# Mixing stage of a hybrid decoder layer: TensorE's order written out, the recurrence's steps spread between the matmuls of products

## The chip, the core and the metric

The kernel runs on one core of a Trainium2 chip, in float32 with three-pass products (below). The metric is the device time of one execution in microseconds, the median of several runs. A profiled execution gives the trace from which every row here comes.

## What is computed

One decoder layer on 1024 tokens of width 1024: a half-step feed-forward layer, a mixing stage, a second feed-forward layer, a gated embedding and a last RMSNorm. The change is in the mixing stage. Its reference, cut:

```
proj = rms(x) @ w_in            # q | f | i | og | pool | gate A | gate B
f = lb + (1 - lb) * sigmoid(f_r);  k = 1 - f;  q = silu(q_r);  v = i_r
S_t = diag(f_t) S_{t-1} + k_t outer v_t;  o_t = S_t^T q_t      # 8 heads, 128x128 state
y_a = (rms_per_head(o) * silu(og)) @ w_branch_a
pooled = trailing mean over 2/4/8/16 tokens - token            # 4 groups of 128 channels
y_b = (pooled @ pool_w * pool_scale) @ w_branch_b
x = x + (sigmoid(ga) * y_a + sigmoid(gb) * y_b) @ w_out
```

## The kernel before

Every product of two float32 matrices is three matmuls on halves of the mantissa (`mm3`: high x high, low x high, high x low; lines 150 to 152), each 128x128 by 128x512. A remainder ("low") is one ScalarE copy (line 118) and one VectorE subtraction (line 119).

The input projection is done in pairs of 128-column blocks (`pair`), by a Strassen-Winograd scheme: seven products instead of eight, each of four `mm3`, so 84 matmuls a pair. `pair` loads the two weight blocks `ra` and `rb`, forms their sums on GpSimd (lines 90 and 93), splits them, and then runs products 1, 2, 6, 5 and 7; products 4 and 3 (`rest`) are kept in `waiting` and run behind products 1 and 2 of the next pair. `qf_pair(h)` makes a head's q and f; `v_pair`, `og_pair`, `gate_pair` and `pool_pair` make two blocks each (two heads' v or output gates, two blocks of a merge gate, two pooling groups), and put them in DRAM.

The recurrence, `hgrn(h, half)`, takes 512 tokens of a head, in four chunks of 128. It computes a chunk's scores by levels 1, 2, 4, ..., 64: at each level eight matmul records of 64 columns (line 837) write a PSUM bank `aux`; VectorE takes parts of it over into the score (`copy_predicated`, line 840; for the two last levels ScalarE, line 848) and multiplies q and k by the decays (line 87), and the next level reads these. Around the levels stand the products of a token with itself (line 810), the transposes of v (817) and k (863), the state products k x v (867), the state's four steps on VectorE (876), the output products (885 and 887), the squares on ScalarE (890), the power on GpSimd (162), the scaling (892), and the transposes of the output (898) with the gate (899).

Tiles come from named rooms: `a` 28 buffers of 1024 columns (the layer's input in its seven forms fills all of them), `w` 12 (weights), `q` 4 (q beside k), `u` 8 of 512 (f and the pairs' outputs), `h` 5 of 512. PSUM has three banks `pA`, one `pB`, one `pC`, three `aux`.

The order of the instructions on each engine isn't written by hand: a planner takes, of what is ready by its own estimate of times, what stands first in the source. All loads and stores are issued by SP's queue. In the source, a head's two calls of `hgrn` follow the pairs that they need, and one or two pairs of `others` follow them:

```
qf_pair(0)
for h in range(HEADS):
    if h < HEADS - 1:
        qf_pair(h + 1)
    if h % 2 == 0:
        v_pair(h)
        og_pair(h)
        flush()
    for half in range(2):
        hgrn(h, half)
    others.pop(0)()
    if h in (1, 3):
        others.pop(0)()
```

Behind the loop the pooled groups `m` are loaded and split, `branch_b(j)` multiplies them by a block of `w_branch_b` and by gate B for j = 0 to 7, `load_act` loads the recurrence's outputs for branch A, and four pairs of `w_branch_a` follow, then the product with `w_out`.

Of the kernel before, what the change touches and what calls it, by code (L numbers as in the profile page):

```python
# [16 lines left out]
P = 128  # L17
# [7 lines left out]
NG = 4  # L25
# [12 lines left out]
def hybrid_block(ctx: ExitStack, tc: tile.TileContext, a: dict, out: bass.AP):  # L38
# [102 lines left out]
    def load(dst, src):  # L141
        nc.sync.dma_start(out=dst, in_=src)
        return dst

    def store(dst, src):
        nc.sync.dma_start(out=dst, in_=src)
# [100 lines left out]
    def norm_act(x, which, tr="aux"):  # L247


        act = new_act()  # L250
        b1 = {}
        g = gains[:, which, :]
        ng = ngains[:, which, :]

        xn = []

        def rows():
            xn.extend(normed_rows(x, range(4)))

        def first():  # L260
            for kc in range(KC):
                ps = turned(xn, kc, tr)
                b1[kc] = t_(("u", "h")[kc >= 6], "b1")
                nc.scalar.mul(b1[kc], ps, g[:, kc : kc + 1])
                if kc % 2:
                    act_first(act, b1[kc - 1], b1[kc])

        def second():
            ts = range(4, 8)
            diag = scales(x, ts)  # L270
            yield
            for kc in range(0, KC, 2):
                p12 = turned_by(x, ts, diag, kc)
                b22 = t_("h", "b22")
                nc.scalar.mul(b22, turned_by(x, ts, diag, kc + 1), g[:, kc + 1 : kc + 2])
                act_second(
                    act, b1[kc], b1[kc + 1], p12, b22, g[:, kc : kc + 1], ng[:, kc : kc + 1]
                )
                yield

        return act, rows, first, second
# [7 lines left out]

    def flush():  # L290
        while waiting:
            waiting.pop(0)()

    def pair(wa, wb, act, tiles, on11, on22, on21, on12, early=False):

        c1, c2, c3 = tiles
        w = {}

        def product(i, ps, start):
            s, b = SIDES[i]
            hi, lo = w[s]
            for k in range(4):
                c = slice(k * P, (k + 1) * P)
                mm3(ps, hi[:, c], lo[:, c], *act[b][k], start and k == 0, k == 3)
# [20 lines left out]
        yield  # L327
        pa, pc = bank("pA"), bank("pC")
        product(1, pa, True)
        nc.scalar.copy(c1, pa)  # L330
        product(2, pc, True)
        add(c1, c1, pc)
        on11(c1)
        yield
        if early:
            sums(raw(wa, "ra"), raw(wb, "rb"))
        yield
        flush()
        pb = bank("pB")
        product(6, pa, False)  # L340
        nc.scalar.copy(c2, pa)  # L341
        product(5, pb, True)
        product(7, pa, False)
        nc.scalar.copy(c3, pa)
        add(c3, c3, pb)
        on22(c3)

        def rest():
            product(4, pa, False)
            on21(pa)  # L350
            product(3, pb, False)
            add(c2, c2, pb)
            on12(c2)

        waiting.append(rest)

    def steps(it, n=9):
        for _ in range(n):
            if next(it, 0) == 0:
                return  # L360
# [4 lines left out]
    def run_pair(*args, **kw):  # L365
        if not starts:
            steps(pair(*args, **kw))
            return
# [52 lines left out]
    def ffn_up(act, w1, w3, gs, after=None):  # L421
        chunk = []

        def one(c):
# [13 lines left out]
            run_pair(  # L438
                w1[c], w3[c], act, (g1, g2, c3),
                silu, lambda t: None, lambda ps: mul(g1, g1, ps), on12,  # L440
            )
# [236 lines left out]
    def qf_pair(h):  # L678
# [18 lines left out]
        run_pair(w_in[Q + h], w_in[F + h], act, (qk[0][:, L], qk[1][:, L], f[1]),  # L697
                 q_(0), f_(1), f_(0), q_(1))

    def out_pair(wa, wb, act_, done):  # L700

        c1, c2, c3, c4 = (t_("u", "o") for _ in range(4))
        run_pair(
# [3 lines left out]
        )  # L707

    def v_pair(h):
# [5 lines left out]
        out_pair(w_in[V + h], w_in[V + h + 1], act, done)  # L715

    def og_pair(h):
        def done(i, half, t, src):
# [7 lines left out]
            store(og_dram[h + i][half], t)  # L726

        out_pair(w_in[OG + h], w_in[OG + h + 1], act, done)

    def gate_pair(at, j, dst):  # L730
# [4 lines left out]
        out_pair(w_in[at + j], w_in[at + j + 1], act, done)  # L735

    pw_split = []

    def pool_group(g, u):
# [3 lines left out]
        while sh < win:  # L743
            nxt = [t_("h", "pw"), t_("h", "pw")]
            for half in range(2):
# [16 lines left out]
        if not pw_split:  # L762
            r = t_("h", "pwr")
            load(r.rearrange("p (g d) -> p g d", g=NG), a["pool_w"].rearrange("g c d -> c g d"))
            pw_split.append(hilo_half(r, "w", "pwhl"))
        wh, wl = pw_split[0]
        gc = slice(g * P, (g + 1) * P)
        for half in range(2):
            ph, pl = hilo_half(u[half], "w", "pb")
            ps = bank("aux")  # L770
            mm3(ps, wh[:, gc], wl[:, gc], ph, pl, True, True)
            nc.scalar.mul(u[half], ps, pscale[:, g : g + 1])
            store(m_dram[g][half], u[half])

    def pool_pair(g):
        got = {}

        def done(i, half, t, src):
# [3 lines left out]
            for k in range(2):  # L782
                if (k, 0) in got and (k, 1) in got:
                    pool_group(g + k, [got.pop((k, 0)), got.pop((k, 1))])

        out_pair(w_in[PU + g], w_in[PU + g + 1], act, done)
# [7 lines left out]
    def hgrn(h, half):  # L794
# [3 lines left out]

        qk, f = heads[h][0][half], heads[h][1][half]
# [16 lines left out]
        for p_, v_ in zip(chunks(ps), chunks(v)):  # L816
            nc.tensor.transpose(p_, v_, ident)
        nc.scalar.copy(v, ps)
# [12 lines left out]
        for hh in LEVELS:  # L831
# [3 lines left out]
            for c in range(4):  # L835
                right = qc[c].rearrange("p (a two h) -> p a two h", two=2, h=hh)[:, :, 1, :]
                nc.tensor.matmul(ps[:m, c, :64], kc[c][:, :m], right, start=True, stop=True)  # L837
            if hh < 32:
# [23 lines left out]
        for p_, a_ in zip(chunks(ps)[:need], kc):  # L862
            nc.tensor.transpose(p_, a_, ident)
        nc.scalar.copy(k[:, : need * P], ps[:, : need * P])
        ps = bank("aux")
        for p_, a_, b_ in zip(chunks(ps)[:need], kc, vc):
            nc.tensor.matmul(p_, a_, b_, start=True, stop=True)
        befores = []
        for c, (s_, p_) in enumerate(zip(chunks(t_("h", "st")), chunks(ps))):
# [13 lines left out]
        for c, p_ in enumerate(chunks(ps)):  # L883
            s_ = befores[c]
            nc.tensor.matmul(p_, sc[:, c, :], vc[c], start=True, stop=s_ is None)
            if s_ is not None:
                nc.tensor.matmul(p_, qc[c], s_, start=False, stop=True)
        rs = const.tile([P, 4], F32, tag="rso", name=name("rso"), bufs=2)
# [7 lines left out]
        ps = bank("aux")  # L896
        for p_, a_ in zip(chunks(ps), qc):
            nc.tensor.transpose(p_, a_, ident)
        nc.vector.scalar_tensor_tensor(og, ps, onorm[:, h : h + 1], og, ALU.mult, ALU.mult)
        store(o_dram[h][half], og)  # L900

    others = [
        lambda: gate_pair(GB, 0, gb_dram), lambda: pool_pair(0),
        lambda: gate_pair(GB, 2, gb_dram), lambda: pool_pair(2),
        lambda: gate_pair(GB, 4, gb_dram), lambda: gate_pair(GB, 6, gb_dram),
        lambda: gate_pair(GA, 0, ga_dram), lambda: gate_pair(GA, 2, ga_dram),
        lambda: gate_pair(GA, 4, ga_dram), lambda: gate_pair(GA, 6, ga_dram),
    ]
    qf_pair(0)
    for h in range(HEADS):  # L910
        if h < HEADS - 1:
            qf_pair(h + 1)
        if h % 2 == 0:
            v_pair(h)
            og_pair(h)
            flush()
        for half in range(2):
            hgrn(h, half)
        others.pop(0)()
        if h in (1, 3):  # L920
            others.pop(0)()


    m_parts = []
    for g in range(NG):
        m = t_("q", "m")
        for half, c in enumerate((L, R)):
            load(m[:, c], m_dram[g][half])
        m_parts.append(halves(hilo(m, "a", "m")))

    BANKS_B = ("aux", "aux", "pA", "aux", "pA")
    n_b = [0]

    def branch_b(j):
        r = load(t_("w", "rw")[:, :HALF], a["w_branch_b"][j])
        wh, wl = hilo_half(r, "w", "wb")
        for half, cols in enumerate((L, R)):
            gb = load(t_("h", "gb"), gb_dram[j][half])
            ps = bank(BANKS_B[n_b[0] % len(BANKS_B)], "yb")
            n_b[0] += 1  # L940
# [3 lines left out]
            t = t_("u", "o")  # L944
            mul(t, ps, gb)
            store(yb_dram[j][half], t)
# [25 lines left out]
    for j in range(KC):  # L972
        branch_b(j)
        if j % 2:
            load_act(j // 2)


    for j in range(0, KC, 2):
# [7 lines left out]
        out_pair(a["w_branch_a"][j], a["w_branch_a"][j + 1], act_a, done)  # L986
# [68 lines left out]
    act = rest_of(x)  # L1055

# [130 lines left out]
```

## Time and profile before

| | |
|---|---|
| median of 3 runs | 2464.32 us (2461.43 to 2470.61) |
| the profiled execution | 2467.48 us, span 2465.8 us, mean granted clock 0.979 |
| TensorE matmuls | busy 2346.3 us (95%) |
| VectorE | busy 1482.6 us (60%) |
| ScalarE | busy 975.2 us (40%) |
| GpSimd | busy 446.4 us (18%) |
| DMA | 334.10 MB, 135 GB/s |

A wide matmul's record lasts longer than the step to the next one, so busy TensorE is not TensorE at its peak. The names in rows: PE is TensorE's matmuls, PEld its weight loads, DVE VectorE, ACT ScalarE, POOL GpSimd, SPq the queue that issues DMAs; L837 is line 837 of the kernel before; `out<-in` are the program's tiles.

### The profile page before, as it was taken

How to read it: one execution, taken by the hardware profiler on the slowest of the kernel's cores; microseconds unless marked ns; L12 is line 12 of the kernel's file. 1: busy time of each engine (PE TensorE's matmuls, PEld its weight loads, DVE VectorE, ACT ScalarE, POOL GpSimd, SP SyncE). 2: the span in 40 equal slices, each digit the busy share in tenths (PEclk: the TensorE clock that was granted, in tenths of full speed). 3: DMA queues.
4: the chain of work that ended last, by engine and by line, in shares of the span. 5: the costliest groups of instructions: out<-in, count | busy, mean ns of one | idle time of the engine just before them, and what ended most of it. 6: DMA issues, size and time to landing. Idle time of an engine off the chain costs nothing.

```text
span 2465.8 us, 29423 instructions
## 1 busy us (share of the span) xinstructions
PE 2346.3 (95%) x11003; PEld 1919.4 (78%) x11003; DVE 1482.6 (60%) x2026; ACT 975.2 (40%) x1511; POOL 446.4 (18%) x390
## 2 busy tenths in 40 slices
PE   8899999999998999989999989999899999999997
PEld 5688788888877778768778767777688888888885
DVE  5745555468565665684564675676645544568558
ACT  7433333333554334243333331236433333334654
POOL 2222232100013112122212201201232222100000
PEclk9999999999999999999999988999999999999998
DMA  5244554574232213122312346663225433663323
GB/s 205 88 160 140 176 179 139 177 277 141 90 121 76 90 48 120 56 98 74 107 59 79 117 149 209 221 219 129 98 90 175 154 124 112 211 246 124 109 101 133
DMA packets 133951, 334.10 MB, mean 135 GB/s; under 512 B 15280, under 2 KB 15792, under 8 KB 133808
## 3 DMA queue, kind: packets, MB, share of 16 engines
q1 hardware_dynamic: 133808, 332.23, 39.1%
q8 instruction: 86, 1.41, 0.2%
q14 instruction: 57, 0.47, 0.1%
HBM read 230.98 MB, written 101.19 MB: 135 GB/s over the span
## 4 chain that ended last, share of the span: by engine, by line
PE 80%; DVE 9%; ACT 3%; issue 3%; POOL 2%; DMA 2%; SPq 0%; DVEq 0%; POOLq 0%; ACTq 0%
PE pA L150 12%; PE pA L151 12%; PE pA L152 12%; PE pB L151 6%; PE pB L150 6%; PE pB L152 6%; PE aux L837 4%; PE pC L151 3%; PE pC L152 3%; PE pC L150 3%; PE aux L151 2%; PE aux L152 2%; PE aux L150 2%; DVE qk L87 1%; DVE tot L87 1%
## 5 line engine op out<-in xcount | busy, mean ns | idle before, releaser
L90 POOL TENSOR_TENSOR s<-rb 128x512 f32<-128x512 f32 x74 | 102.4, 1384 | 736.2 <-PE pA L152 359.7
L119 DVE TENSOR_TENSOR wtl<-rb,wth 128x1024 fp32r<-128x1024 f32 x74 | 90.7, 1225 | 152.2 <-ACT wth L118 151.8
L118 ACT CAST wsh<-s 128x1024 fp32r<-128x1024 f32 x74 | 77.8, 1051 | 231.0 <-POOL s L93 219.5
L93 POOL TENSOR_TENSOR rb<-ra,s 128x512 f32<-128x512 f32 x74 | 96.4, 1303 | 382.0 <-DVE wd L119 382.0
L837 PEld LDWEIGHTS aux<-qk 128*128 128x128 f32 (+1 forms) x896 | 107.2, 189 | 44.8 <-issue 28.2
L118 ACT CAST wth<-rb 128x1024 fp32r<-128x1024 f32 x74 | 77.6, 1048 | 155.4 <-POOL rb L93 155.4
L118 ACT CAST gh<-gr 128x1024 fp32r<-128x1024 f32 x84 | 81.8, 980 | 135.8 <-PE aux L151 86.4
L118 ACT CAST wah<-ra 128x1024 fp32r<-128x1024 f32 x74 | 77.9, 1052 | 134.9 <-PE pC L151 81.3
L837 PE MATMUL aux<-qk 128*128 128x64 f32 (+1 forms) x896 | 114.5, 272 | 17.4 <-DVE qk L87 16.5
L119 DVE TENSOR_TENSOR gl<-gr,gh 128x1024 fp32r<-128x1024 f32 x84 | 94.8, 1132 | 59.8 <-ACT gh L118 59.7
L150 PE MATMUL pA<-xT1h,wsh 128*128 128x512 f32 x280 | 111.9, 400 | 19.8 <-ACT xT1h L118 19.8
L119 DVE TENSOR_TENSOR wsl<-s,wsh 128x1024 fp32r<-128x1024 f32 x74 | 91.0, 1230 | 61.8 <-ACT wsh L118 50.4
L150 PE MATMUL pA<-xT3h,wth 128*128 128x512 f32 x296 | 118.1, 399 | 4.2 <-ACT g L341 3.2
L150 PE MATMUL pB<-xT1h,wsh 128*128 128x512 f32 x296 | 117.1, 396 | 1.8 <-ACT xT1h L118 0.9
L150 PE MATMUL pC<-x0h,wah 128*128 128x512 f32 x296 | 117.0, 395 | 1.5 <-ACT x0h L118 1.3
L152 PE MATMUL pA<-x0h,wal 128*128 128x512 f32 x296 | 116.7, 394 | 1.6 <-DVE wal L119 1.6
L152 PE MATMUL pB<-xT1h,wsl 128*128 128x512 f32 x296 | 117.9, 398 | 0.0
L151 PE MATMUL pC<-x0l,wah 128*128 128x512 f32 x296 | 116.8, 394 | 1.0 <-DVE x0l L119 1.0
L151 PE MATMUL pB<-xT1l,wsh 128*128 128x512 f32 x296 | 117.0, 395 | 0.4 <-DVE xT1l L119 0.4
L150 PE MATMUL pA<-x0h,wah 128*128 128x512 f32 x296 | 117.2, 396 | 0.0
L151 PE MATMUL pA<-xT3l,wth 128*128 128x512 f32 x296 | 117.0, 395 | 0.0
L152 PE MATMUL pA<-xT3h,wtl 128*128 128x512 f32 x296 | 117.0, 395 | 0.0
(338 smaller groups left out, 6580.6 us busy)
## 6 DMA issues: line engine op xcount, KB each, us to landing
ra<-in_ffn_w_dram SPq DMA_DIRECT2D x50, 512.0 KB, 3.7
rb<-in_ffn_w_dram SPq DMA_DIRECT2D x44, 512.0 KB, 4.0
gsS<-gs SPq DMA_DIRECT2D x88, 256.0 KB, 2.1
rB<-in_ffn_w_dram SPq DMA_DIRECT2D x40, 512.0 KB, 6.7
gr<-gsS SPq DMA_DIRECT2D x40, 512.0 KB, 3.5
gsA<-g SPq DMA_DIRECT2D x66, 256.0 KB, 2.0
gr<-gsA SPq DMA_DIRECT2D x30, 512.0 KB, 5.1
ra<-in_w_in_dram SPq DMA_DIRECT2D x29, 512.0 KB, 3.6
```

The source lines that it names most:

```text
L87: nc.vector.tensor_tensor(o, x, y, ALU.mult)
L90: nc.gpsimd.tensor_tensor(o, x, y, ALU.add)
L93: nc.gpsimd.tensor_tensor(o, x, y, ALU.subtract)
L118: nc.scalar.copy(hi, src)
L119: nc.vector.tensor_tensor(lo, src, hi.bitcast(F32), ALU.subtract)
L150: nc.tensor.matmul(ps, ah, bh, start=first, stop=False, **kw)
L151: nc.tensor.matmul(ps, ah, bl, start=False, stop=False, **kw)
L152: nc.tensor.matmul(ps, al, bh, start=False, stop=last, **kw)
L837: nc.tensor.matmul(ps[:m, c, :64], kc[c][:, :m], right, start=True, stop=True)
```

## The change

`pair`, `run_pair` and the functions that call them become generators: they stop (`yield False`) behind each of a product's four `mm3`, a "part" of three matmuls. `hgrn` stops behind each of its groups of matmuls, twelve in a half. For each head, `among` draws parts from the pairs that `more` names, so many per group, and within `tc.manual_schedule(engines={nc.tensor.engine})` TensorE's instructions keep the order of the source. The other engines' order stays the planner's.

The pairs are dealt out anew: v, qf and og of head 0 before the loop; in heads 0 and 2 a pooling pair, the next qf pair, the pooling maps and a gate pair; in heads 1, 3 and 5 the next head's v, qf and og; in heads 4 and 6 the next qf pair and two gate pairs; in head 7 two gate pairs and the first column of branch B. The pooling means are taken a step at a time behind each part of a qf pair, in `w` buffers; the maps follow as parts of their own. v of a half is loaded in the half in front of it, behind its eighth group; og of a half behind its state products. The states go into f's tile. The last transposes of a half (`turn`) come behind the third group of the next half. Loads can be queued on SP behind a named transfer (`issue_after`).

```diff
+    behind, latest = [None], [None]
+    def load(dst, src, at_once=False):
+        with ExitStack() as turn:
+            if behind[0] is not None and not at_once:
+                turn.enter_context(tc.issue_after(behind[0]))
+            latest[0] = nc.sync.dma_start(out=dst, in_=src).ins
         return dst
...
             for k in range(4):
                 c = slice(k * P, (k + 1) * P)
                 mm3(ps, hi[:, c], lo[:, c], *act[b][k], start and k == 0, k == 3)
+                yield False
...
-    def pool_group(g, u):
+    def beside_means(it):
+        for part in it:
+            yield part
+            while means and next(means[0], 0) == 0:
+                means.pop(0)
+        while means:
+            for _ in means.pop(0):
+                pass
+
+    def pool_means(g, u):
...
-            nxt = [t_("h", "pw"), t_("h", "pw")]
+            both = t_("w", "pw")
+            nxt = [both[:, L], both[:, R]]
             for half in range(2):
...
                     add(n[:, :sh], c[:, :sh], cur[0][:, HALF - sh :])
+                yield
...
+    def v_of(h, half):
+        return v_next.pop() if v_next else v_load(h, half)
...
-        v = load(t_("h", "v"), v_dram[h][half])
-        og = load(t_("h", "og"), og_dram[h][half])
+        v = v_of(h, half)
 
         ps = bank("aux")
         for p_, k_, q_ in zip(chunks(ps), kc, qc):
             nc.tensor.matmul(p_, k_, q_, start=True, stop=True)
+        yield
...
+        og = load(t_("h", "og"), og_dram[h][half], True)
+        og_last[0] = latest[0]
         befores = []
-        for c, (s_, p_) in enumerate(zip(chunks(t_("h", "st")), chunks(ps))):
+
+        for c, (s_, p_) in enumerate(zip(chunks(f), chunks(ps))):
...
+        def turn():
+            ps = bank("aux")
+            for p_, a_ in zip(chunks(ps), qc):
+                nc.tensor.transpose(p_, a_, ident)
+            nc.vector.scalar_tensor_tensor(og, ps, onorm[:, h : h + 1], og, ALU.mult, ALU.mult)
+            store(o_dram[h][half], og)
+
+        turns.append(turn)
+
+    GROUPS = 2 * 13
+
+    def head(h):
         for half in range(2):
-            hgrn(h, half)
+            for i, _ in enumerate(hgrn(h, half)):
+                if i == 2 and turns:
+                    turns.pop(0)()
+                if i == 7:
+                    at = 2 * h + half + 1
+                    if at < 2 * HEADS:
+                        v_next.append(v_load(at // 2, at % 2))
+                yield
+
+    def among(its, groups, n):
+        parts = (p for it in its for p in it if not p)
+        done = 0
+        for i, _ in enumerate(groups, 1):
+            while done * GROUPS < i * n:
+                next(parts, None)
+                done += 1
+        for _ in parts:
+            pass
+
+    PAIR = 28
...
+    more = {
+        0: lambda: (pool_pair(0), beside_means(qf_pair(1)), pool_maps(),
+                    gate_pair(GB, 0, gb_dram)),
+        2: lambda: (pool_pair(2), beside_means(qf_pair(3)), pool_maps(),
+                    gate_pair(GB, 2, gb_dram)),
+        4: lambda: (qf_pair(5), gate_pair(GB, 4, gb_dram), gate_pair(GB, 6, gb_dram)),
+        6: lambda: (qf_pair(7), gate_pair(GA, 0, ga_dram), gate_pair(GA, 2, ga_dram)),
+        7: lambda: around(gate_pair(GA, 4, ga_dram), act_b(), gate_pair(GA, 6, ga_dram), flushed(),
+                          branch_b(0)),
+    }
...
+    with tc.manual_schedule(engines={nc.tensor.engine}):
+        for h in range(HEADS):
+            its = more[h]() if h in more else (v_pair(h + 1), qf_pair(h + 1), og_pair(h + 1))
+            among(its, head(h), (74 if h == 7 else 3 * PAIR + 4 * (h in (0, 2))))
+        turns.pop(0)()
+    behind[0] = og_last[0]
...
-    for j in range(KC):
-        branch_b(j)
+    for j in range(1, KC):
+        steps(branch_b(j))
         if j % 2:
             load_act(j // 2)
+    behind[0] = latest[0]
```

## Rows read from the trace of the kernel before

**Rows 1.** The page: busy us (share of the span) and instructions of each engine.

```profile
PE 2346.3 (95%) x11003; PEld 1919.4 (78%) x11003; DVE 1482.6 (60%) x2026; ACT 975.2 (40%) x1511; POOL 446.4 (18%) x390
```

**Rows 2.** Timeline of PE, 790 to 840: start us, us, instruction, how many.

```profile
793.22 0.39 PE L150 MATMUL pA<-xT1h,wsh 128*128 128x512 f32 x1
...
801.15 0.39 PE L152 MATMUL pA<-xT3h,wtl 128*128 128x512 f32 x1
...
821.95 0.40 PE L151 MATMUL pB<-xT1l,wsh 128*128 128x512 f32 x1
822.18 1.00 PE L837 MATMUL aux<-qk 128*128 128x64 f32 x8
822.99 0.48 PE L152 MATMUL pB<-xT1h,wsl 128*128 128x512 f32 x1
823.31 0.39 PE L150 MATMUL pB<-xT1h,wsh 128*128 128x512 f32 x1
...
824.45 1.02 PE L837 MATMUL aux<-qk 128*128 128x64 f32 x8
...
828.35 0.39 PE L152 MATMUL pA<-xT3h,wtl 128*128 128x512 f32 x1
...
834.65 0.39 PE L151 MATMUL pA<-x0l,wah 128*128 128x512 f32 x1
...
837.93 0.63 PE L898 MATMUL aux<-ident,qk 128*128 128x128 f32 x4 [0.82 <-DVE tot L87]
...
839.96 0.40 PE L150 MATMUL pC<-x0h,wah 128*128 128x512 f32 x1
```

**Rows 3.** Windows: length; busy (count) PE, PEld, DVE, ACT, POOL; clock, DMA, GB/s.

```profile
801.38:1493.62 692.24, 643.28 (x3490) 529.73 (x3489) 432.68 (x732) 247.26 (x489) 135.65 (x101) 0.98 0.28 91
1403.60:1431.71 28.11, 27.14 (x167) 22.57 (x166) 20.73 (x38) 12.82 (x27) 1.01 (x1) 1.00 0.58 187
1459.80:1493.62 33.82, 22.32 (x102) 19.38 (x101) 20.88 (x38) 8.63 (x19) 1.01 (x1) 0.55 0.28 94
1321.00:1374.00 53.00, 52.40 (x236) 43.37 (x235) 22.39 (x28) 20.39 (x29) 11.88 (x10) 1.00 0.33 104
```

**Rows 4.** The same windows, only instructions on tile aux (PE, PEld, DVE, ACT).

```profile
801.38:1493.62 692.24, 212.54 (x1584) 193.21 (x1583) 97.45 (x183) 55.22 (x216) 0.98 0.28 91
1403.60:1431.71 28.11, 12.17 (x99) 11.31 (x98) 5.99 (x11) 3.09 (x13) 1.00 0.58 187
1459.80:1493.62 33.82, 20.90 (x99) 18.69 (x97) 5.96 (x11) 3.08 (x13) 0.55 0.28 94
```

**Rows 5.** Waits of PE, 740 to 1640: us in total, times, longest.

```profile
PE aux L837 <- DVE qk L87: 16.5, 17, 1.4
PE aux L898 <- DVE qk L892: 15.6, 11, 3.5
...
PE pA L150 <- ACT xT1h L118: 5.9, 1, 5.9
...
PE aux L817 <- DMA v<-v_dram: 1.2, 1, 1.2
```

**Rows 6.** Timeline of DVE around the level group at 822.18.

```profile
823.22 0.44 DVE L840 COPY_PREDICATED score<-mask,aux 128x256 f32<-128x256 uint16 x1 [1.50 <-PE aux L837]
823.56 0.68 DVE L87 TENSOR_TENSOR qk<-qk,tot 128x512 f32<-128x512 f32 x1
```

**Rows 7.** Groups by line, 600 to 1800: busy us, mean ns; idle before.

```profile
L119 DVE TENSOR_TENSOR wtl<-rb,wth 128x1024 fp32r<-128x1024 f32 x34 | 41.6, 1224 | 56.0 <-ACT wth L118 55.6
```

**Rows 8.** DMA issues, 740 to 1500: count, KB each, median us to landing.

```profile
v<-v_dram SPq DMA_DIRECT2D x16, 256.0 KB, 3.0
```

**Rows 9.** Timeline of DVE in a pooling group.

```profile
1066.13 0.68 DVE L81 TENSOR_TENSOR pw<-o 128x511 f32<-128x511 f32 x1
...
1068.81 0.68 DVE L81 TENSOR_TENSOR pw<-pw 128x508 f32<-128x508 f32 x1
```

**Rows 10.** Waits of all engines, 740 to 1640: us in total, times, longest.

```profile
POOL rso L162 <- DVE rso L161: 134.0, 10, 32.7
```

More of the change, by code (lines that the diff above doesn't have):

```diff
@@ L288, in hybrid_block, with flushed @@
     waiting = []
+    def flushed():
+        while waiting:
+            yield from waiting.pop(0)()
     def flush():
-        while waiting:
-            waiting.pop(0)()
+        for _ in flushed():
+            pass
     def pair(wa, wb, act, tiles, on11, on22, on21, on12, early=False):
@@ L348, in rest @@
         def rest():
-            product(4, pa, False)
+            yield from product(4, pa, False)
             on21(pa)
-            product(3, pb, False)
+            yield from product(3, pb, False)
             add(c2, c2, pb)
@@ L357, in steps @@
     def steps(it, n=9):
-        for _ in range(n):
-            if next(it, 0) == 0:
+        for end in it:
+            n -= end
+            if not n:
                 return
@@ L366, in run_pair @@
         if not starts:
-            steps(pair(*args, **kw))
+            yield from pair(*args, **kw)
             return
@@ L702, in out_pair @@
         c1, c2, c3, c4 = (t_("u", "o") for _ in range(4))
-        run_pair(
+        yield from run_pair(
             wa, wb, act_, (c1, c2, c3),
@@ L707, in out_pair @@
         )
+    v_there = set()
     def v_pair(h):
@@ L713, in done @@
             store(v_dram[h + i][half], t)
-        out_pair(w_in[V + h], w_in[V + h + 1], act, done)
+            v_there.add((h + i, half))
+        yield from out_pair(w_in[V + h], w_in[V + h + 1], act, done)
+    og_there, og_last = set(), [None]
     def og_pair(h):
@@ L726, in done @@
             store(og_dram[h + i][half], t)
-        out_pair(w_in[OG + h], w_in[OG + h + 1], act, done)
+            og_there.add((h + i, half))
+        yield from out_pair(w_in[OG + h], w_in[OG + h + 1], act, done)
     def gate_pair(at, j, dst):
@@ L761, in pool_group, with pool_maps @@
             )
[L762 to L773, printed above, removed]
+            yield
+        pooled.append((g, u))
+    def pool_maps():
+        r = t_("h", "pwr")
+        load(r.rearrange("p (g d) -> p g d", g=NG), a["pool_w"].rearrange("g c d -> c g d"))
+        wh, wl = hilo_half(r, "w", "pwhl")
+        while pooled:
+            g, u = pooled.pop(0)
+            gc = slice(g * P, (g + 1) * P)
+            for half in range(2):
+                ph, pl = hilo_half(u[half], "w", "pb")
+                ps = bank("aux")
+                mm3(ps, wh[:, gc], wl[:, gc], ph, pl, True, True)
+                nc.scalar.mul(u[half], ps, pscale[:, g : g + 1])
+                store(m_dram[g][half], u[half])
+                yield False
     def pool_pair(g):
@@ L783, in done, with v_load @@
                 if (k, 0) in got and (k, 1) in got:
-                    pool_group(g + k, [got.pop((k, 0)), got.pop((k, 1))])
-        out_pair(w_in[PU + g], w_in[PU + g + 1], act, done)
+                    means.append(pool_means(g + k, [got.pop((k, 0)), got.pop((k, 1))]))
+        yield from out_pair(w_in[PU + g], w_in[PU + g + 1], act, done)
+    v_next = []
+    def v_load(h, half):
+        assert (h, half) in v_there
+        return load(t_("h", "v"), v_dram[h][half], True)
+    def v_of(h, half):
+        return v_next.pop() if v_next else v_load(h, half)
     states = {}
@@ L895, in hgrn @@
         )
[L896 to L916, printed above, removed]
-        for half in range(2):
-            hgrn(h, half)
-        others.pop(0)()
-        if h in (1, 3):
-            others.pop(0)()
-    m_parts = []
[L925 to L929, printed above, removed]
@@ new lines, in among, with around @@
+    def among(its, groups, n):
[6 more added lines that the diff above has]
+        for _ in parts:
+            pass
+    PAIR = 28
+    def around(first, acts, *its):
+        yield first
+        next(acts)
+        for it in its[:-1]:
+            yield it
+        next(acts)
+        yield its[-1]
+    more = {
[8 more added lines that the diff above has]
+    }
@@ L934, in branch_b, with act_b @@
+    for it in (v_pair(0), qf_pair(0), og_pair(0)):
+        steps(it)
+    m_parts = []
+    def act_b():
+        behind[0] = latest[0]
+        for g in range(NG):
+            m = t_("q", "m")
+            for half, c in enumerate((L, R)):
+                load(m[:, c], m_dram[g][half])
+            m_parts.append(halves(hilo(m, "a", "m")))
+        m_last, behind[0] = latest[0], None
+        yield True
+        behind[0] = m_last
+        yield True
     def branch_b(j):
@@ L937, in branch_b @@
         for half, cols in enumerate((L, R)):
-            gb = load(t_("h", "gb"), gb_dram[j][half])
-            ps = bank(BANKS_B[n_b[0] % len(BANKS_B)], "yb")
-            n_b[0] += 1
+            gb = load(t_("u", "gb"), gb_dram[j][half])
+            ps = bank("pA", "yb")
             for i, g in enumerate((0, 2, 1, 3)):
@@ L943, in branch_b @@
                 mm3(ps, wh[:, c], wl[:, c], *m_parts[g][half], i == 0, i == 3)
-            t = t_("u", "o")
-            mul(t, ps, gb)
-            store(yb_dram[j][half], t)
+                yield False
+            mul(gb, ps, gb)
+            store(yb_dram[j][half], gb)
+    with tc.manual_schedule(engines={nc.tensor.engine}):
[4 more added lines that the diff above has]
+    behind[0] = og_last[0]
     act_a = new_act()
@@ L1055, in hybrid_block @@
     act = rest_of(x)
+    behind[0] = None
     ffn_up(act, a["ffn2_w1"], a["ffn2_w3"], gs_dram,
```

50 lines of the change are left out of this document (28 added, 22 removed).

## The prediction

> **What bounds the kernel now.** The page first: TensorE counts as busy for 95% of the span, VectorE for 60% [rows 1]. Read alone, that leaves 5% to win anywhere. A matmul's record is longer than its pace, though, so I went on to the pace. Where pairs run alone, 36 matmuls of 512 columns start from 793.22 to 801.15, a step of 0.2266 us, while each record says 0.39 [rows 2]; two neighbours can drift apart by 0.16 us and still count as busy. [...]
>
> Then the windows. With pairs alone (1321 to 1374) nothing is lost: 236 matmuls x 0.2266 = 53.5 us for 53.0 [rows 3]. The mixing with the recurrence is another thing. From its first matmul (801.38) to its last (1493.62) are 692.2 us and 3490 matmuls, of which 1584 write aux [rows 3, 4]. 24 of these are pooling maps, which are as wide as the pairs', so 1560 are the recurrence's and about 1930 are wide ones. 1930 x 0.2266 = 437 us. The other **255 us** are what the recurrence's 16 halves cost TensorE, 15.9 each.
>
> How much of that is work? I price one half from the timeline where it runs without idle time [rows 2]. One level group (8 records): from the wide matmul at 821.95 to the second one after it, 823.31, are 1.36, less two steps 0.91. The transposes and first products at a half's start: 837.93 to 839.96, less one step: 1.80. From the last level to the state products, 828.35 to 834.65: 6.30 less the 11 wide matmuls in it (2.49): 3.81. A half is 6 x 0.91 + 1.80 + 3.81 = **11.1 us**, 16 halves 177. So 255 - 177 = **78 us** of the stretch are waits, lost pace and slow clock. [...] A well filled half is the one from 1403.60: 28.1 us, 167 matmuls, 68 of them wide = 15.4, so 12.7 for the recurrence. If all were like it: 203, and 52 us saved.
>
> The waits that TensorE's own list names are the recurrence's: 16.5 us for VectorE's multiply between levels, 15.6 for the normalised output before its transposes [rows 5].
>
> **The change, part by part.** *Order and even spreading.* No matmul is added or taken away. A half has 12 stops for other work; `among` lays 84 parts of three wide matmuls (88 with the maps, 74 counted for the last head) over 26 per head, 3.2 parts between two groups and the rest at the head's end: 3.2 x 3 x 0.2266 = 2.2 us. Does the chain fit into that? After the group at 822.18 the next wide matmul starts at 822.99; VectorE's select starts at 823.22, its multiply ends at 824.24, and the next group starts at 824.45 [rows 2, 6]: 1.46 us. So 0.74 us are spare where VectorE is free. [...] Were everything to fit, the gain would be the 78.
>
> What doesn't fit: VectorE's 1.22 us remainders of weights [rows 7], three per pair, 69 in the 23 pairs of the loop. Against a period of 3.1 us one of them lies in front of the multiply by more than 0.74 now and then: if it gets between select and multiply (0.44 of 3.1) it costs 1.22 - 0.74 = 0.48, if it is running when the select comes due, 0.09 on the mean (0.39 of the time). That is 0.10 x 69 = 7; two such instructions in a row happen, so I take 13. Ends: nothing, and 69 x 0.48 = 33.
>
> *The turn* (transposes of the output) moves to the third group of the next half, 9 us later instead of at once; the chain of squares, power on GpSimd and multiply, of which 3.5 us were the longest wait seen [rows 5], goes under that. The very last one has no cover: 3.
>
> *v a half ahead.* It lands 3.0 us after issue [rows 8]; TensorE waited 1.2 for it, once [rows 5]. The load moves on SP's queue past a half's stores, and its source was stored by the head's first pair long before; og moves back, behind the state products, with a whole gap and three groups until its use. Both at nothing beyond the 1.2, which is in the 78; without that cover, 3.0 per half would show.
>
> *State in f's tile.* Four chunks per half leave the h buffers, but f lives to the end of its head. Two heads' f and an output pair's four tiles fill the eight u buffers; the next pair's first copy needs only the buffer whose store went out a pair ago. Nothing, I estimate.
>
> *Pooling in steps.* A step is one add, 0.67 us apart from the next (1066.13 to 1068.81 for four) [rows 9]; the four groups have 20, and some 1.4 more each, 19 us in all. One step per part asks VectorE for 0.67 beside the pair's 0.285 (22.39 us for 236/3 parts [rows 3]) and the recurrence's 1.19 per group ((20.73 - 22.7 x 0.285)/12) x 0.3 = 0.36: 1.31 us in a part that lasts 0.68 + 0.3 x 0.91 = 0.95. VectorE falls behind by 0.36 over 26 such parts, 9 us; I take 8. Ends: nothing, and all 19. The maps at the end wait some 4 for the last steps.
>
> *Loads behind others.* m's loads, branch B's and branch A's are queued behind a named transfer. Branch A's weights then come only after the last o, some 12 us after the loop; 4 for landing and some 11 for sums and casts end before branch B's seven remaining columns (168 x 0.2266 = 38 us) do. Nothing; without the cover, what exceeds 38.
>
> Sum: 177 + 13 + 3 + 8 + 4 = 205 against 255: **50 us saved**. The profiled execution took 2467.5 us (span 2465.8), 3 above the median of the runs; from the median, 2464.3 - 50 = **2414**.
>
> **Rivals.** *VectorE gives it back.* All three upper ends together: 177 + 33 + 19 + 7 = 236, 19 saved, 2445. For it: VectorE is busy 432.7 of the 692 us already and will have the same work in 640, 68% [rows 3]. Against it: the well filled half runs at 20.73/28.1 = 74% and loses 1.6 us only.
>
> *Slower: GpSimd's queue holds the weights.* The power of each half stands on GpSimd among the sums of the pairs' weights. GpSimd now waits 134 us in ten such places, up to 32.7 at once [rows 10], and TensorE doesn't feel it, since the recurrence's own groups or another pair stand in its order. With the order fixed, a pair whose sums stand behind the power stops recurrence and pairs alike. At 16 powers, 50/16 = 3.1 us each eat the gain; at the 5.9 that TensorE once waited for a cast [rows 5] it is 94: 2464 - 50 + 94 = 2508. Against it: the recurrence's results come at a steady pace, and a pair lasts 26 us instead of 19, so that its sums have 7 more to hide in. [...]
>
> *Nothing happens.* The order by readiness already filled the gaps, and idle time only moves: 2464. Against it: the last half spends 33.8 less three wide matmuls = 33.1 us on the recurrence, 20 more than the well filled one, and the pairs now placed there must change that.
>
> **How the numbers follow.** Forecast, 2390 to 2435 (nothing but the floor, to stalls of 49 in place of 28): 0.62. VectorE gives it back, 2435 to 2455: 0.18. Nothing: 0.08. Slower: 0.12. Half a per cent, 12 us, is about what a measurement of this kernel can tell. Faster by more, under 2452: 0.62 + 0.17 = 0.79; within: 0.01 + 0.08 and 0.01 of the slower case, 0.10; slower: 0.11. The floor is 2464 - 78 = 2386. From 2390 to 2452 hold about 8 in 10.
>
> **What would show it.** Right: the recurrence's groups spread evenly from its first to its last matmul in about 640 us and no half at the low clock; the wait for the normalised output gone; small waits on VectorE's multiply, most of them in the pooling pairs. Wrong: waits of TensorE for casts of weights with GpSimd's power ahead of them; waits for the level multiply at most groups, a microsecond each; or idle time of 10 us and more where branch A begins.

## The result and the profile after

The changed kernel takes **2433.36 us** (median of 4 runs, 2428.49 to 2434.36) against 2463.81 (2461.43 to 2470.61): ratio 0.9868, interval 0.9844 to 0.9892, 30.5 us less. The forecast was 2414, in a range from 2390 to 2452. The profiled executions are 33.7 apart, 2467.48 and 2433.77, since that of before lies above its median.

TensorE's busy time, as the page gives it (compare [rows 1]), fell by 13 us and its share rose by one per cent; it tells little here, as before.

```profile
PE 2333.1 (96%) x11003; PEld 1914.5 (79%) x11003; DVE 1479.2 (61%) x2027; ACT 976.3 (40%) x1512; POOL 446.7 (18%) x390
```

The windows tell more. Line 1 is the stretch from the recurrence's first matmul to its last, as in [rows 3]; then its first half, head 0's second half (pooling), head 2's second half (pooling), a plain half, and the last. The columns are those of [rows 3].

```profile
786.19:1460.28 674.09, 648.98 (x3566) 542.39 (x3564) 430.10 (x731) 249.51 (x496) 141.59 (x105) 0.99 0.28 92
786.19:830.65 44.46, 40.63 (x219) 34.09 (x217) 24.59 (x48) 13.64 (x28) 6.70 (x6) 0.96 0.23 71
830.65:878.53 47.88, 44.29 (x239) 36.63 (x238) 36.00 (x66) 20.26 (x40) 13.04 (x10) 1.00 0.28 94
999.27:1053.89 54.62, 48.22 (x239) 38.34 (x238) 42.41 (x82) 20.19 (x40) 15.01 (x10) 0.94 0.25 83
1092.95:1135.36 42.41, 42.06 (x233) 35.43 (x232) 23.45 (x35) 14.84 (x30) 12.39 (x10) 1.00 0.16 56
1416.02:1460.28 44.26, 39.25 (x214) 32.31 (x212) 31.69 (x48) 19.76 (x38) 1.58 (x2) 0.96 0.64 213
```

Of 3566 matmuls 1560 are the recurrence's, as before, so 2006 are wide: 454.6 us at 0.2266. What is left, called the remainder below, is 674.1 - 454.6 = **220 us** (219.5; 220.0 when each half is taken by itself). It was 255; the forecast had 205, of which 177 are work. The same sum for single halves, with 97 or so matmuls of the recurrence in each:

| half | remainder, us | over the 11.1 of work |
|---|---|---|
| first (786.19) | 16.6 | 5.5 |
| head 0, second (pooling) | 15.9 | 4.9 |
| head 2, second (pooling) | 22.7 | 11.6 |
| last (1416.02) | 19.1 | 8.0 |
| the other twelve, mean | 12.1 (11.4 to 12.6) | 1.0 |

The last half, which cost 33 us when it stood bare, costs 19; the plain ones are at 12.1 on the mean, and of before none was under 12.7. The waits of PE from 730 to 1640 answer to [rows 5]: total, times, longest.

```profile
PE aux L886 <- DVE qk L87: 11.6, 15, 2.7
PE pA L157 <- ACT xT1h L118: 7.4, 2, 4.6
PE aux L865 <- DMA v<-v_dram: 3.8, 1, 3.8
...
PE aux L158 <- DVE pb L119: 2.4, 1, 2.4
...
PE aux L957 <- DVE qk L949: 0.6, 1, 0.6
```

The 15.6 us for the normalised output are 0.6 now. Those for the level multiply are still 11.6, but 8.8 of these stand in the two pooling halves and the last one. The wait for v, 1.2 before, is 3.8. GpSimd waits longer for the power's operand than before ([rows 10]), with no wait of TensorE for a weight behind it in the loop; total, times, longest, from 780 to 1462:

```profile
POOL rso L169 <- DVE rso L168: 170.4, 16, 41.4
```

Outside the stretch the profiled executions differ by little. One pair (84 matmuls, 19.0 us) has moved from ahead of the recurrence into it, and it begins only 15.2 us earlier, so 3.8 were lost there; behind it are 2.4 gained. 35.1 - 3.8 + 2.4 = 33.7.

### The profile page after: what moved, and what is told of

It is laid out like the page before. It is cut to its first block, busy times and chain, and to the rows that moved or that the text cites. A ratio compares the mean times of both kernels' runs of the same rounds, so it can differ in the third digit from the quotient of the medians.

```text
span 2432.0 us, 29361 instructions
## 1 busy us (share of the span) xinstructions
PE 2333.1 (96%) x11003; PEld 1914.5 (79%) x11003; DVE 1479.2 (61%) x2027; ACT 976.3 (40%) x1512; POOL 446.7 (18%) x390
## 4 chain that ended last, share of the span: by engine, by line
PE 75%; DVE 10%; DMA 5%; ACT 3%; issue 3%; POOL 2%; SPq 0%; DVEq 0%; POOLq 0%; ACTq 0%
PE pA L157 12%; PE pA L158 12%; PE pA L159 12%; PE pB L157 6%; PE pB L158 6%; PE pB L159 5%; PE aux L886 3%; PE pC L158 3%; PE pC L159 3%; PE pC L157 3%; PE aux L158 2%; PE aux L159 2%; PE aux L157 2%; DMA rb<-in_ffn_w_dram 1%; DVE tot L87 1%
## 5 line engine op out<-in xcount | busy, mean ns | idle before, releaser
L157 PE MATMUL pA<-xT1h,wsh 128*128 128x512 f32 x280 | 115.5, 412 | 21.4 <-ACT xT1h L118 21.4
L886 PE MATMUL aux<-qk 128*128 128x64 f32 (+1 forms) x896 | 110.4, 266 | 16.3 <-DVE qk L87 11.6
L157 PE MATMUL pB<-x,wth 128*128 128x512 f32 x296 | 118.1, 399 | 0.0
L158 PE MATMUL pA<-x0l,wah 128*128 128x512 f32 x296 | 115.6, 391 | 2.4 <-DVE x0l L119 2.4
L159 PE MATMUL pC<-x0h,wal 128*128 128x512 f32 x296 | 116.6, 394 | 0.0
```

The lines of the kernel that those rows point to most:

```text
L157: nc.tensor.matmul(ps, ah, bh, start=first, stop=False, **kw)
L158: nc.tensor.matmul(ps, ah, bl, start=False, stop=False, **kw)
L159: nc.tensor.matmul(ps, al, bh, start=False, stop=last, **kw)
```

## The experiments

The times are medians; where a ratio stands, it is that to the kernel before, timed beside it. Remainders are computed as above, with 454.6 us for the wide matmuls.

**The fixed order taken away.**

```diff
-    with tc.manual_schedule(engines={nc.tensor.engine}):
+    with ExitStack():
```

> The changed kernel, but TensorE's order is left to the planner again; source, spreading, pairs, loads and pooling steps stay as changed. If the even spreading in the source does the work and the fixed order only holds it, the planner, which takes what stands first in the source of what is ready, comes close to the same order: time within 6 us of the changed kernel's 2433, remainder of the recurrence (stretch from its first to its last matmul less 0.2266 us per wide matmul) 214 to 226 against 220. If the fixed order itself does it, the planner draws the recurrence's groups together again: remainder back towards 255, time some 2465.

Measured: 2419.19, ratio 0.982 (0.9805 to 0.9834): 14 us *faster* than with the fixed order, outside both expectations. Windows: the stretch, head 2's second half, the last half; and the wait for v.

```profile
785.26:1444.49 659.23, 641.82 (x3566) 538.04 (x3565) 434.45 (x732) 250.83 (x496) 139.47 (x105) 1.00 0.29 95
993.30:1043.10 49.80, 45.17 (x239) 36.09 (x238) 43.65 (x82) 20.38 (x40) 13.16 (x10) 1.00 0.26 91
1402.91:1444.49 41.58, 37.77 (x214) 31.12 (x213) 31.82 (x49) 20.34 (x38) 1.58 (x2) 1.00 0.72 235
```

```profile
PE aux L865 <- DMA v<-v_dram: 1.2, 1, 1.2
```

The remainder is 204.6. The plain halves are what they were (12.0). The difference is in the disturbed ones: the first 16.6 to 12.4, pooling 22.7 to 17.9 and 15.9 to 15.2, the last 19.1 to 16.2. At the first half one can see how. In the changed kernel, v is late and TensorE stands:

```profile
789.59 0.39 PE L159 MATMUL pA<-x0h,wal 128*128 128x512 f32 x1
793.81 0.77 PE L865 MATMUL aux<-ident,v 128*128 128x128 f32 x4 [3.83 <-DMA v<-v_dram]
794.23 0.78 PE L157 MATMUL pC<-x0h,wah 128*128 128x512 f32 x1
794.80 0.63 PE L158 MATMUL pC<-x0l,wah 128*128 128x512 f32 x1
...
797.36 0.52 PE L158 MATMUL pC<-x0l,wah 128*128 128x512 f32 x1
```

The planner put ten more wide matmuls in front of the transposes, the last of them at 790.92, and the wait is 1.2:

```profile
788.65 0.39 PE L159 MATMUL pA<-x0h,wal 128*128 128x512 f32 x1
788.88 0.39 PE L157 MATMUL pC<-x0h,wah 128*128 128x512 f32 x1
...
790.92 0.39 PE L157 MATMUL pC<-x0h,wah 128*128 128x512 f32 x1
792.50 0.66 PE L865 MATMUL aux<-ident,v 128*128 128x128 f32 x4 [1.20 <-DMA v<-v_dram]
```

**Groups close together, in the fixed order and in the planner's.**

```diff
-    GROUPS = 2 * 13
+    GROUPS = 2 * 22
```

> The changed kernel with the parts of a head laid over 44 instead of 26 groups: 1.9 parts (1.30 us) between two groups instead of 3.2 (2.2 us), the other 38 parts of a head behind its last group. If cover for the chain of 1.46 us between two level groups is what the change bought, TensorE waits at most level groups, 0.16 at the least and up to 1.2 where VectorE is at a weight's remainder: remainder of the recurrence 250 to 265 against 220, time 2460 to 2475. If the filled last head and the fixed order bought it and the spacing doesn't matter, remainder 215 to 227 and 2428 to 2440.

> TensorE's order left to the planner and a head's parts laid over 44 groups (1.30 us between two, less than the chain's 1.46). If spacing is what counts whoever makes the order, the stretch's remainder rises from 205 to between 225 and 255 and the time to 2440 to 2470. If the planner makes up for close groups by putting later parts between them, the remainder stays under 213 and the time under 2427.

Measured: 2475.88 fixed, 2434.46 by the planner (one run each). The stretch of each, and the fixed one's longest wait:

```profile
783.14:1497.42 714.28, 664.36 (x3566) 550.91 (x3564) 429.78 (x729) 248.67 (x494) 137.38 (x105) 0.97 0.26 86
```

```profile
786.56:1458.96 672.40, 649.10 (x3566) 538.88 (x3564) 427.88 (x729) 248.01 (x494) 140.47 (x105) 0.99 0.28 90
```

```profile
PE aux L886 <- DVE qk L87: 31.6, 29, 3.2
```

Remainders 259.7 and 217.8, against 219.5 and 204.6 with 2.2 us between groups. So 0.9 us of cover per group are worth 40 us where the order is fixed and 13 where the planner makes it. The first remainder lies in the range that I had worked out from the chain of 1.46 us (250 to 265; the time is 0.9 above its range), but not by the waits that I had in mind: not 0.16 at most groups, but 31.6 us in 29 of the 112 level groups, up to 3.2 at once. The second fell between my two expectations: the planner makes up for two thirds.

**The transposes of the output earlier.**

```diff
-                if i == 2 and turns:
+                if i == 0 and turns:
```

> The changed kernel with the last transposes of a half behind the first group of the next half instead of the third: 3.1 us of cover instead of 9 within a head (some 7.5 at a head's start). If their place is worth what the prediction says, TensorE waits about 1 us for the normalised output in each of eight halves and more where GpSimd or VectorE is busy: 8 to 15 us slower, 2441 to 2448, and the wait for the scaling (line 949) comes back at 8 to 15 us. If their place doesn't matter: within 2 us of the changed kernel.

Measured: 2433.70, ratio 0.9877 (0.986 to 0.9893), no change in time. The waits moved in the way expected, by less:

```profile
PE aux L886 <- DVE qk L87: 14.5, 22, 1.2
...
PE aux L957 <- DVE qk L949: 4.7, 9, 1.6
```

4.7 us in nine waits came back where I expected 8 to 15. The plain halves grew by 0.6 on the mean, 7 us in all, but the last half and one of the pooling halves became shorter by 3.3 together, the stretch as a whole is 3.4 longer, and the time doesn't show it. The place of the turn is worth some microseconds at most.

**No pooling means.**

```diff
-                    means.append(pool_means(g + k, [got.pop((k, 0)), got.pop((k, 1))]))
+                    pooled.append((g + k, [got.pop((k, 0)), got.pop((k, 1))]))
```

> The changed kernel without the pooling means (the pooling maps are applied to the tokens themselves; all else is done). If the means' steps on VectorE make the long halves of heads 0 and 2, these halves' remainders fall from 15.9 and 22.7 to 12.5 and 15, the stretch by 11 us: 2422. If the splits of the maps (five pairs of copies and subtractions close together) make them, the halves keep 15 and 20 and the time falls by 3 at most.

Measured: 2422.58, ratio 0.983 (0.9816 to 0.9845), as the first theory says, 11 us. The pooling halves have remainders of 13.6 and 13.6 (12.5 and 15 expected), 11.4 less together, and what they keep over a plain half, 1.5 each, goes with the maps and their splits. The first half fell too, by 2.4: its wait for v was 3.0 there, and the granted clock of the whole stretch is 1.00 where it was 0.99.

**The means in a lump.**

```diff
-            while means and next(means[0], 0) == 0:
-                means.pop(0)
+            while means:
+                for _ in means.pop(0):
+                    pass
```

> The changed kernel, fixed order, with a pooling group's means taken all at once in the source instead of a step behind each part. If the steps ease VectorE's load, the long halves of heads 0 and 2 grow from 15.9 and 22.7 us to 18 and 28, the time to 2441. If VectorE is overloaded there in either way and works through what stands first in the source, both stay within 1.5 us, the time within 4 of 2433.

Measured: 2431.80 (one run); the pooling halves have 17.0 and 24.3, 1.1 and 1.6 more, and the first half and the last differ by 0.8 together. The stretch is 3.3 us longer, though the time of this one run isn't. That is nearer to the second theory, with 1.6 just past its 1.5: the steps ease little, VectorE is overloaded there either way.

**v in its own half, in the fixed order and in the planner's.**

```diff
-                    if at < 2 * HEADS:
+                    if False:
                         v_next.append(v_load(at // 2, at % 2))
```

> The changed kernel, fixed order, with v loaded at its own half's start as before. If SP issues the load about when the half's first group is reached, 3 us of transfer and queue stand against some 3 us of cover, and TensorE waits about a microsecond for v in most of the 16 halves: 10 to 25 us slower, 2443 to 2458. If SP runs far enough ahead that a load early in the source lands early anyway: within 3 us of 2433, and the waits for v stay at the 3.8 us of the first half.

> TensorE's order left to the planner, and v loaded at its own half's start. With the fixed order this cost 16 us, in four halves where TensorE waited up to 3.7 us for v. If what the fixed order costs is that nothing can be taken in front of a late operand, the planner hides most of it: these halves rise by 2 at most, the time is under 2425. If v is late whatever the order: 2432 to 2438.

Measured: 2449.38 fixed, ratio 0.9937 (0.992 to 0.9955); 2425.92 by the planner, ratio 0.9836 (0.9813 to 0.9859). The first is 16 us slower by the medians, as the first theory says (the profiled execution, the fastest of the four, 11.1), but TensorE waits for v in four halves, not in most: the first ones of heads 0, 2, 4 and 6. Head 4's first half, fixed and by the planner, and the waits for v of each:

```profile
1137.51:1181.48 43.97, 40.00 (x216) 33.20 (x215) 27.29 (x50) 15.27 (x30) 6.43 (x6) 0.96 0.34 103
```

```profile
1128.84:1169.88 41.04, 39.50 (x217) 33.43 (x216) 26.61 (x50) 15.26 (x30) 6.05 (x6) 0.96 0.35 110
```

```profile
PE aux L865 <- DMA v<-v_dram: 14.3, 4, 3.7
```

```profile
PE aux L865 <- DMA v<-v_dram: 6.7, 4, 1.9
```

With v a half ahead these halves have 12.0 and 11.2; late, 17.5 and 14.5. The fixed order pays 5.5 for it, the planner's 3.3, so it hides less than I expected (2 at most), and its time lies between my two theories.

**Another order of the pairs ahead of the loop**, by the planner and fixed.

```diff
-    for it in (v_pair(0), qf_pair(0), og_pair(0)):
+    for it in (qf_pair(0), og_pair(0), v_pair(0)):
```

> TensorE's order left to the planner, the three pairs before the loop in the order qf, og, v, the means back on VectorE alone. If the two gains add up, the recurrence begins some 6 us earlier than with the planner's order alone (779 against 785), its stretch keeps a remainder of 203 to 206, and the time is 2410 to 2415, 5 to 8 under the 2419. If the earlier start is given back later: 2417 to 2421.

> The changed kernel, fixed order, with the three pairs before the loop in the order qf, og, v. If the late first v (3.8 us) and what it does to the clock are only a part of what the fixed order costs, the first half falls to some 12 us, the recurrence begins 6 us earlier, the pooling halves and the last one stay at 16, 22.7 and 19: 2421 to 2427, still 8 to 13 over the same pairs with the planner's order (2414). If the first v is all of it: 2412 to 2418.

Measured: 2413.72 (5 runs, 2411.86 to 2418.41), ratio 0.9799 (0.9785 to 0.9814), by the planner, and 2420.81, ratio 0.9818 (0.9798 to 0.9839), fixed. The first is as expected; the second is 0.2 under its range, and 7 over the planner's where I had expected 8 to 13. The recurrence begins at 779.88 and 778.86 instead of 785 to 786; v is in time, and the first half's remainder is 11.0 in both. The stretches:

```profile
779.88:1437.54 657.66, 641.56 (x3566) 538.27 (x3565) 430.98 (x722) 249.32 (x494) 139.52 (x105) 1.00 0.30 95
```

```profile
778.86:1446.83 667.97, 647.26 (x3566) 541.68 (x3564) 428.71 (x720) 247.84 (x493) 139.03 (x105) 0.99 0.29 93
```

The new order of the pairs is worth 12.6 us where TensorE's order is fixed and 5.5 where it isn't, so that about half of what the fixed order costs hung on the start. The intervals of the ratios overlap, for the 5.5 as for the 7 us that remain, so these are less sure than the 14 above; the two stretches are 10.3 apart, of which 8 are in the pooling halves (16.0 and 22.2 against 15.2 and 18.0) and the last (19.0 against 15.9). The planner's order with these pairs beats both kernels; it is the best that I have.

**Half of the means on GpSimd, and no parts left at a head's end** (both by the planner, with the pairs in the order qf, og, v).

```diff
-                add(n[:, sh:], c[:, sh:], c[:, :-sh])
+                (pool_add if half else add)(n[:, sh:], c[:, sh:], c[:, :-sh])
```

```diff
-    GROUPS = 2 * 13
+    GROUPS = 2 * 12
```

> TensorE's order left to the planner, the three pairs before the loop in the order qf, og, v, and the wide adds of the second half's means on GpSimd. Against the run with the planner's order alone (2419): the pairs' order gives back the 3.8 us that the changed kernel lost before the loop, if its last pair's gate work on ScalarE and VectorE made that; the means on GpSimd take 7 adds, some 4.7 us, off VectorE in the half of 17.9, which falls by 3 to 5, and by 1 or 2 in the half of 15.2: 2408 to 2413. If GpSimd's adds (1.4 us each) come later than VectorE's would, these halves grow instead, to 20 and more.

> The kernel with the planner's order, the pairs in the order qf, og, v and half of the means on GpSimd, and besides a head's parts laid over 24 groups, as many as there are, instead of 26: 3.5 parts (2.38 us) between two groups, none left at a head's end. If what still waits in the plain halves is VectorE's long instructions against 0.74 us of spare, 0.18 more of it takes 2 to 5 us off the stretch. If the remaining 12 us per half are work, and the spare is enough already, within 1 us; and if the bare parts at a head's end covered the last transposes, 2 to 5 slower.

Measured: 2416.48, ratio 0.9799 (0.9784 to 0.9815), and 2416.25, ratio 0.9801 (0.9785 to 0.9816). The means on GpSimd are a miss: 2408 to 2413 were expected. Head 0's second half kept its 15.2, head 2's rose from 18.0 to 21.4, as the other theory has it, and TensorE waits for means there that it did not wait for before. 24 groups or 26 make no difference: remainders of 207.2 and 207.5. By what I had written down, that would clear VectorE's long instructions in the plain halves; why it settles little is told in the next section.

## Why the prediction was right, and where it was off

The direction held, and the mechanism in the main. The stretch lost waits, lost pace and slow clock, not work; the recurrence is spread evenly; the last half no longer stands bare; the cover between two groups counts, which the close groups show: with 0.16 us less than the chain of 1.46 the fixed order's remainder is 260, where 255 was before. It isn't all of it: with the same close groups the planner's order keeps only 218, 37 less than before, and spreading takes 13 more. So under the planner the greater part came with the new deal of pairs and loads, 21 of it in the last half alone (33 to 12.4); what each piece of that deal brought was not measured by itself. GpSimd's queue, the rival on the other side, did not decide: its waits for the power grew from 134 to 170 us, and no weight was late in the loop. Long VectorE instructions go with GpSimd's sums, which is another matter, told below.

The size was off by 20 us: 50 forecast, 30.5 measured. Three of these lie between the medians and the profiled executions, which are 33.7 apart. The other 16 are in the terms of the sum, over the 177 of work:

| term | forecast | measured |
|---|---|---|
| VectorE's long instructions; measured, all that the plain halves keep | 13 | 12.5 |
| pooling steps and maps | 8 + 4 | 16.5 |
| the end (last turn) | 3 | 8.0 |
| v ("at nothing beyond the 1.2"), first half | 0 | 5.5 |
| ahead of the recurrence | 0 | 3.8 |
| behind it | 0 | -2.4 |

The first row agrees to half a microsecond, and that is luck. The forecast's cause was a weight's remainder in front of the multiply between levels. But in the twelve plain halves TensorE's list has only 5.7 us of waits, 13 of them. The rest of the 12.5 is lost pace, or work that I priced too low; no run parts the two, and the half from 959.99, with no idle time at all, still has 11.4. Of the 5.7 us, 4.6 stand behind VectorE instructions that were long beside something that I had overlooked, GpSimd's sums of weights. A multiply or another product of 512 columns (L87) took 0.67 to 0.74 us in 142 of the 158 cases in the stretch and 1.00 to 1.74 in 16. Each of the 16 started while GpSimd was adding, and ended 0.55 us after that add did. TensorE's waits for VectorE from 1054 to 1416 (nine of the twelve halves; total, times, longest), then two places, each with VectorE, GpSimd and the wait of TensorE:

```profile
PE aux L886 <- DVE qk L87: 2.4, 8, 0.4
PE aux L886 <- DVE tot L87: 1.8, 2, 0.9
...
1270.00 1.74 DVE L87 TENSOR_TENSOR qk<-qk,tot 128x512 f32<-128x512 f32 x1
1269.89 1.30 POOL L93 TENSOR_TENSOR rb<-ra,s 128x512 f32<-128x512 f32 x1 [7.75 <-DVE wd L119]
1271.88 1.08 PE L886 MATMUL aux<-qk 128*128 128x64 f32 x8 [0.34 <-DVE qk L87]
...
1229.16 3.77 DVE L87 TENSOR_TENSOR tot<-tot 128x128 f32<-128x128 f32 x3
1228.82 1.44 POOL L90 TENSOR_TENSOR s<-rb 128x512 f32<-128x512 f32 x1 [11.98 <-PE pA L159]
1230.34 1.29 POOL L93 TENSOR_TENSOR s<-s,ra 128x512 f32<-128x512 f32 x1
1231.59 1.29 POOL L93 TENSOR_TENSOR rb<-ra,rb 128x512 f32<-128x512 f32 x1
1234.01 1.08 PE L886 MATMUL aux<-qk 128*128 128x64 f32 x8 [0.92 <-DVE tot L87]
```

The three small products in the second place (128, 64 and 32 columns) took 0.29, 0.22 and 0.19 us where GpSimd was not adding. Five waits are of the first kind (1.8 us), three of the second (2.7). Eight products of 512 columns started during an add and took 0.68 to 0.74, and no run moved the sums away, so what they cost in all is open. The run with 24 groups doesn't settle it: with the greater cover, TensorE's waits for the multiply between levels were 8.8 us in eight, where they were 4.8 in ten with 26 groups.

The step of the prediction that failed is the one that reckoned the fixed order as a gain alone ("Order and even spreading"). It lists what the spreading buys and charges nothing for holding TensorE to one order. Without the hold the kernel is 14 us faster, at the same source and the same spreading. The remainders put it together (close groups by the planner: one run): new deal of pairs and loads with close groups, by the planner, 255 to 218; even spreading, to 205; the fixed order, back to 220. My second rival did charge the fixed order, but looked for the cost in the wrong place, at GpSimd's power. The halves in which the fixed order costs are those with a late operand: the first v, the pooling maps' splits, and in the last half what waits for VectorE beside its work on m.

v failed in its own right. "Past a half's stores" on SP's queue was right for 15 of the 16 loads. The first has no half in front of it, and stands behind two weight loads, which wait for GpSimd to be done with a weight buffer. What SP waits for most from 760 to 800 (total, times, longest), and its issues in the changed kernel:

```profile
SPq L149 <- POOL rb L93: 15.5, 2, 12.8
...
786.25 0.33 SPq L149 DMA_DIRECT2D ra<-in_w_in_dram  x1
788.59 0.33 SPq L149 DMA_DIRECT2D rb<-in_w_in_dram  x1
788.97 0.42 SPq L149 DMA_DIRECT2D v<-v_dram  x1
```

SP had issued nothing since 770.24. v goes out at 788.97, and the transposes at 793.81 are the first that can use it. A queue that the load is moved past was looked at for the usual half, not for the first one.

Of pooling I had priced the steps and not the splits behind them: five remainders of 0.68 us on VectorE around 1018 to 1022, one of which TensorE awaits for 2.4. The run without means puts 11.4 us on the steps, where I had 8 and 4. The lump agrees with my picture of the deficit (0.36 us per part) in kind: steps or lump, the work is too much for the time. In the last half I had not listed the four splits of m at all; the longest wait there, 2.7 us, is for the first level's multiply, and VectorE's timeline has two of these splits in front of it, the second itself behind a cast:

```profile
1423.19 1.26 DVE L119 TENSOR_TENSOR ml<-m,mh 128x1024 fp32r<-128x1024 f32 x1
1424.36 0.75 DVE L958 SCALAR_TENSOR_TENSOR og<-aux,onorm,og 128x512 f32<-128x512 f32 x1
1425.93 1.23 DVE L119 TENSOR_TENSOR ml<-m,mh 128x1024 fp32r<-128x1024 f32 x1 [0.82 <-ACT mh L118]
1427.08 0.69 DVE L87 TENSOR_TENSOR qk<-qk,f 128x512 f32<-128x512 f32 x1
```

The 3.8 us ahead of the recurrence have to do with the order of the first three pairs, since another order recovers them; which of these pairs' instructions delays the casts there, I did not separate.

## What to carry to other kernels

Where a chain on one engine alternates with another's work, find the chain's shortest turn (here 1.46 us) and lay a little more cover than that between its steps in the source; that alone was worth 13 us under a planner that may still reorder, and 40 under a fixed order. Look also at what GpSimd does while the chain's VectorE steps run: here one of 0.68 us took up to 1.74 when it started during an add. Try the spreading without the fixed order first: a planner that takes the next thing in the source when one operand is late keeps the gain and loses less at the irregular places, at the start, at the end, and where another stage overloads an engine. When a load is moved ahead, follow it on its queue for the first iteration too.

## What the runs showed of the hardware

After the 3.8 us stand for v (789.59 is the last matmul before it), wide matmuls started 0.43 us apart until 797.4 instead of 0.23. The granted clock was 1.00 up to the stand and in it (785.0 to 793.8) and 0.56 on the mean from 793.8 to 797.4; in windows of 0.4 us it reads 0.50 all the way from 794.6 to 797.4, and 1.00 again from 797.8. With the other pairs ahead of the loop, fixed order and no wait, that half has 11.0 instead of 16.6, so the wait cost 5.6: its own 3.8 and 1.8 of slow steps. With v in its own half, TensorE waited for v in four halves, up to 3.7 us at once; head 4's first half, one of them, has a granted clock of 0.96 on the mean, as the changed kernel's first half, and grew by 5.5. The clock didn't fall every time. In the changed kernel it was 0.50 to 0.51 over 3.3 to 3.5 us from 1019.5, 1033.15 and 1429.1, each 0.3 to 1.8 us after a wait of 2.4, 2.2 or 2.7 had ended; behind waits of 2.4 and 2.6 that ended at 1504.96 and 1580.56 it stayed at 1.00 for the next 4 us.

With half of the means on GpSimd, some small VectorE instructions took far longer: copies of 2 to 8 columns, 158 to 163 ns in the kernel before, have a median of 1002. A wide add on GpSimd took 1406 against VectorE's 680. Duration ns min/median/max of the tile `pw` in that run:

```profile
L90 POOL TENSOR_TENSOR pw<-pw x6: 1320/1406/1548, 820.2 to 1000.7; 128x510 f32<-128x510 f32 x3, 128x508 f32<-128x508 f32 x2, 128x504 f32<-128x504 f32 x1
L780 DVE COPY pw<-pw x6: 158/1002/1004, 820.7 to 1002.5; 128x2 f32<-128x2 f32 x3, 128x4 f32<-128x4 f32 x2, 128x8 f32<-128x8 f32 x1
```

In the changed kernel the long instructions lie beside the adds. Of the 24 products of 512 columns that started during a GpSimd add, 16 took 1.00 to 1.74 us and ended 0.55 after it, and eight took 0.68 to 0.74. Of the 48 products of 128, 64 and 32 columns, 13 took 1.17 to 1.30, each of them overlapping an add, and the others 0.18 to 0.29. That the copies above were long for the same reason is my inference, and what decides which instruction is long was not tested.
